# PSUM chunks as one run, a convolution that reads PSUM, and low weight parts kept in DRAM

## The chip, the cores and the metric

One core of one Trainium2 chip. The metric is the device time of one execution in microseconds (us). The engines are named as in the profile: PE (TensorE matmul), PEld (TensorE weight load), DVE (VectorE), ACT (ScalarE), POOL (GpSimd), SP (SyncE, which issues nearly all DMAs here).

## What is computed

One step of a two-layer backbone of width 1024 over 128 context tokens and 1024 latent tokens. Layer 0 mixes tokens by attention and pooling, layer 1 by a Conformer convolution module. Each layer ends with a ConvFFN of inner width 2816: a product with `w_in` (1024 x 5632), a depthwise convolution over three tokens, a gate, a product with `w_out`. All of it is fp32.

```python
def conformer_conv(h, w_pw1, dw_w, dw_b, ln_g, ln_b, w_pw2):
    u = h @ w_pw1
    a, g = jnp.split(u, 2, axis=-1)
    u = a * jax.nn.sigmoid(g)
    u = dwconv(u, dw_w, dw_b)                       # 31 taps
    u = jax.nn.silu(layernorm(u, ln_g, ln_b))
    return u @ w_pw2

def conv_ffn(h, w_in, conv_w, conv_b, w_out):
    u = dwconv(h @ w_in, conv_w, conv_b)            # 3 taps
    a, g = jnp.split(u, 2, axis=-1)
    return (jax.nn.silu(a) * g) @ w_out

for i in range(DEPTH):                              # 2; mc/ml: adaLN shift, scale, gate
    ...
    hl = rmsnorm(xl, norm_mix[i]) * (1 + ml[1]) + ml[0]
    yl = ...                                        # attention + pooling, or conformer_conv
    xl = xl + ml[2] * yl
    hl = rmsnorm(xl, norm_ffn[i]) * (1 + ml[4]) + ml[3]
    xl = xl + ml[5] * conv_ffn(hl, ffn_w_in[i], ffn_conv_w[i], ffn_conv_b[i], ffn_w_out[i])
    # the same for the context tokens xc with mc
```

## The kernel before

Activations lie feature-major: eight tiles `x` of 128 features by 1154 token columns (128 context, a gap of 2, 1024 latent). After layer 0's mixer the work goes over two ranges of columns, A (up to 664 columns) and B (some 490 to 512), each an object of class `Part`. A range of more than 512 columns is cut into `n = 2` equal chunks of `cw` columns, since a matmul writes at most 512 columns here; each chunk begins at the start of its own bank of a two-bank PSUM tile `mm`, so its columns have a hole in the middle. A range of one chunk uses a one-bank tile `mn` where such a pool is open.

Products are exact to about fp32 by splitting: a weight *unit* of 128 x 1024 is loaded as `wraw` by SP, ACT copies it to `whi` in the matmul format fp32r, and POOL subtracts to get the low part `wlo = wraw - whi` (`wunit`, L248 and L249). `wraw` has two buffers, `whi` and `wlo` three. `mm3` then issues three products for each slice: hi x hi (L256), hi x lo (L258), lo x hi (L260). `inproj` makes one such product over eight slices into one PSUM tile.

The feed-forward (`ffn`) runs once for each layer and range. `conv(f)` makes one of 44 inner tiles: ACT evacuates the PSUM tile twice, as a copy `fu` (L1066) and as the middle tap `facc` (L1067), and DVE adds the outer taps from `fu` in SBUF (L1068, L1069). `pair` makes the gated tile: SiLU (L1075), product (L1078: DVE in range A, POOL in range B), hi copy `fh` (L1081, ACT) and low part `fl` (L1082, DVE). `out` takes two gated tiles and two units of `w_out` and goes over eight output tiles; `residual` adds each to `x` by DVE reading PSUM (L428), one instruction for each stretch of columns that `pieces` gives: a stretch ends at the border between context and latent tokens and at the border of a chunk. The order is conv, conv, the output phase of the pair before, conv, conv.

Beside these run other chains, interleaved by generators at written rates: in layer 0's range A the modulation of layer 1 (`mod_beside`: loads `mraw` into one buffer and accumulates on DVE, L314 and L316); in layer 0's range B and in the first part of layer 1's range A the Conformer's 31 taps (`dwconv`: a few taps by ACT and POOL, L963 and L964, the others by DVE, L975) and its gated units (`glu`, L931 to L946). PSUM pools change on the way: three two-bank tiles in layer 0's range A and layer 1's range A, one two-bank and five one-bank tiles in most of layer 0's range B, seven one-bank tiles in layer 1's range B.

Nothing orders engines by hand: the framework's scheduler simulates a timeline and fixes each engine's order, SP's DMAs included, and adds the waits; a tile is free for its next writer when its last reader is done.

## Time and profile before

| | |
|---|---|
| median of 3 runs | 2956.2 us (2955.88 to 2958.3) |
| the profiled execution | 2959.12 us, its span 2957.3 us |
| granted TensorE clock, mean | 0.959 |
| busy: PE, DVE, POOL, ACT | 2702.6, 2088.6, 1428.2, 1162.7 us |
| HBM read, written | 257.36 MB, 12.07 MB |
| L249, the low weight parts (POOL) | 346 instructions, 899.7 us |
| L1068 and L1069, the outer taps (DVE) | 352 instructions, 442.3 us |
| L1066, the copy `fu` (ACT) | 176 instructions, 112.2 us |

Busy times are sums over the span, in which the stages differ; the granted clock is the share of full speed that the TensorE's throttle gave. A group's line in the profile gives count, busy time, mean length of one instruction, and after the bar the idle time just before them with what ended it.

### The profile page before, as it was taken

What the parts mean: (1) busy time and instruction counts of PE and PEld (TensorE: products, weight loads), DVE (VectorE), ACT (ScalarE), POOL (GpSimd) and SP (SyncE); (2) the same over time, 40 slices, a digit from 0 to 9 for tenths busy, and PEclk for the clock granted to TensorE, in tenths of its full rate; (3) what the DMA queues carried; (4) which work ended last, traced back from release to release, by engine and by line L of the source; (5) the groups of instructions that cost most, each with busy time, mean ns of one, the idle gap of its engine ahead of it and who ended that gap; (6) DMA issues with size and microseconds to landing.
All of it is one profiled execution on the core that took longest, in us unless ns stands there. A gap on an engine that the chain in (4) does not pass through costs nothing.

```text
span 2957.3 us, 38873 instructions
## 1 busy us (share of the span) xinstructions
PE 2702.6 (91%) x15108; PEld 2419.7 (82%) x15108; DVE 2088.6 (71%) x2850; ACT 1162.7 (39%) x1807; POOL 1428.2 (48%) x752
## 2 busy tenths in 40 slices
PE   8999997989999999997777799986879999999999
PEld 6798885869998998886666688976778999988887
DVE  3146777677768687859998987679997755754444
ACT  3326665324422332544334243534232423433343
POOL 1313334344423323566657675686563634445554
PEclk9999998989999999998988899998889999999999
DMA  6621225432333333221111222221112222233332
GB/s 244 209 58 59 53 75 154 156 127 80 99 108 107 107 108 121 79 86 57 57 55 60 73 85 79 79 79 44 57 44 73 71 79 82 86 112 100 93 97 88
DMA packets 111897, 271.96 MB, mean 92 GB/s; under 512 B 42849, under 2 KB 48097, under 8 KB 111713
## 3 DMA queue, kind: packets, MB, share of 16 engines
q1 hardware_dynamic: 111712, 269.47, 29.5%
q8 instruction: 120, 1.97, 0.3%
q14 instruction: 65, 0.52, 0.1%
HBM read 257.36 MB, written 12.07 MB: 91 GB/s over the span
## 4 chain that ended last, share of the span: by engine, by line
PE 54%; DVE 34%; DMA 5%; ACT 3%; issue 2%; POOL 2%; SPq 0%; POOLq 0%; DVEq 0%; ACTq 0%
DVE acc L975 13%; PE mm L256 8%; PE mm L258 8%; PE mm L260 8%; PE mn L256 5%; PE mn L258 5%; PE mn L260 5%; DVE modacc L316 4%; DMA mraw<-in_wmod_dram 4%; DVE facc L1068 3%; DVE x L428 3%; DVE facc L1069 2%; PE mm L445 2%; PE O L875 1%; DVE fl L1082 1%
## 5 line engine op out<-in xcount | busy, mean ns | idle before, releaser
L249 POOL TENSOR_TENSOR wlo<-wraw,whi 128x1024 fp32r<-128x1024 f32 x346 | 899.7, 2606 | 1007.9 <-ACT whi L248 815.6
L256 PE MATMUL mm<-h,whi 128*128 128x332 f32 (+6 forms) x2208 | 563.6, 326 | 28.7 <-DVE x L428 9.8
L248 ACT ACTIVATE whi<-wraw 128x1024 fp32r<-128x1024 f32 x348 | 363.1, 1053 | 559.2 <-PE mm L258 262.4
L260 PE MATMUL mm<-h,wlo 128*128 128x332 f32 (+6 forms) x2208 | 564.6, 326 | 9.3 <-POOL wlo L249 9.2
L258 PE MATMUL mm<-h,whi 128*128 128x332 f32 (+6 forms) x2208 | 563.4, 326 | 0.0
L1068 DVE SCALAR_TENSOR_TENSOR facc<-fu,params,facc 128x663 f32<-128x663 f32 (+3 forms) x176 | 262.1, 1489 | 337.6 <-ACT facc L1067 337.6
L975 DVE SCALAR_TENSOR_TENSOR acc<-u,params,acc 128x661 f32<-128x661 f32 (+1 forms) x376 | 484.9, 1312 | 19.2 <-POOL acc L964 15.1
L256 PEld LDWEIGHTS mm<-h,whi 128*128 128x128 f32 x2208 | 385.0, 191 | 47.4 <-issue 25.4
L260 PEld LDWEIGHTS mm<-h,wlo 128*128 128x128 f32 x2208 | 384.5, 190 | 22.9 <-POOL wlo L249 11.4
L258 PEld LDWEIGHTS mm<-h,whi 128*128 128x128 f32 x2208 | 383.2, 190 | 12.2 <-issue 1.7
L428 DVE SCALAR_TENSOR_TENSOR x<-mm,mod,x 128x128 f32<-128x128 f32 (+7 forms) x600 | 233.2, 445 | 70.7 <-PE mm L260 70.0
L260 PE MATMUL mn<-h,wlo 128*128 128x494 f32 (+1 forms) x672 | 262.5, 394 | 15.5 <-POOL wlo L249 15.5
L256 PE MATMUL mn<-h,whi 128*128 128x494 f32 (+1 forms) x672 | 264.6, 394 | 4.8 <-ACT whi L248 4.2
L258 PE MATMUL mn<-h,whi 128*128 128x494 f32 (+1 forms) x672 | 263.8, 393 | 0.0
L256 PE MATMUL mm<-fh,whi 128*128 128x332 f32 (+2 forms) x720 | 180.3, 332 | 65.9 <-ACT fh L1081 32.7
L316 DVE SCALAR_TENSOR_TENSOR modacc<-mraw,sc,modacc 128x512 f32<-128x512 f32 x168 | 173.7, 1086 | 68.8 <-DMA mraw<-in_wmod_dram 68.8
L964 POOL TENSOR_TENSOR acc<-acc,tap 128x508 f32<-128x508 f32 (+1 forms) x104 | 186.3, 1795 | 26.9 <-ACT tap L963 23.8
L1081 ACT ACTIVATE fh<-facc 128x664 fp32r<-128x664 f32 (+3 forms) x88 | 60.4, 686 | 335.0 <-DVE facc L1078 215.2
L256 PEld LDWEIGHTS mm<-fh,whi 128*128 128x128 f32 x720 | 127.0, 198 | 77.3 <-ACT fh L1081 33.9
L258 PE MATMUL mm<-fl,whi 128*128 128x332 f32 (+2 forms) x720 | 178.1, 328 | 9.4 <-DVE fl L1082 9.4
L1069 DVE SCALAR_TENSOR_TENSOR facc<-fu,params,facc 128x663 f32<-128x663 f32 (+3 forms) x176 | 180.2, 1024 | 3.3
L256 PE MATMUL mn<-fh,whi 128*128 128x512 f32 (+1 forms) x336 | 135.0, 420 | 50.2 <-ACT whi L248 24.3
(224 smaller groups left out, 4573.4 us busy)
## 6 DMA issues: line engine op xcount, KB each, us to landing
wraw<-in_fi_dram SPq DMA_DIRECT2D x176, 512.0 KB
mraw<-in_wmod_dram SPq DMA_DIRECT2D x96, 512.0 KB
wraw<-in_fo_dram SPq DMA_DIRECT2D x88, 512.0 KB
wraw<-in_pw_dram SPq DMA_DIRECT2D x48, 512.0 KB
x<-in_x_dram SPq DMA_DIRECT2D x16, 577.0 KB
wraw<-in_woab_dram SPq DMA_DIRECT2D x16, 512.0 KB
wraw<-in_wab_dram SPq DMA_DIRECT2D x12, 512.0 KB
wraw<-in_wv_dram SPq DMA_DIRECT2D x8, 512.0 KB
```

The source lines that it names most:

```text
L248: nc.scalar.activation(hi, raw, AF.Copy)
L249: (eng or nc.gpsimd).tensor_tensor(lo, raw, hi.bitcast(F32), op=ALU.subtract)
L256: mm(pv, whi, xhi[:, a:b], start=start, stop=False)
L258: mm(pv, whi, xlo[:, a:b], start=False, stop=False)
L260: mm(pv, wlo, xhi[:, a:b], start=False, stop=stop)
L316: i = nc.vector.scalar_tensor_tensor(acc, rv, c, acc, op0=ALU.mult, op1=ALU.add)
L428: nc.vector.scalar_tensor_tensor(xd[:, a:b], pv, gate[:, d, st:st + 1], xd[:, a:b], op0=ALU.mult, op1=ALU.add)
L964: nc.gpsimd.tensor_tensor(acc[:, :n], acc[:, :n], p[:, :n], op=ALU.add)
L975: nc.vector.scalar_tensor_tensor(acc[:, :n], u[:, t:t + n], wk(i, t), acc[:, :n], op0=ALU.mult, op1=ALU.add)
L1068: nc.vector.scalar_tensor_tensor(acc[:, 1:W], u[:, 0:W - 1], w(0), acc[:, 1:W], op0=ALU.mult, op1=ALU.add)
L1069: nc.vector.scalar_tensor_tensor(acc[:, 0:W - 1], u[:, 1:W], w(2), acc[:, 0:W - 1], op0=ALU.mult, op1=ALU.add)
L1081: nc.scalar.activation(hi[:, :W], a[:, :W], AF.Copy)
```

## The change

Three things are edited.

1. Chunks as one run. `Part.ps` places the first chunk at the end of bank 0 and the second at the start of bank 1, so that a range's columns lie without a hole; `pieces` then yields one stretch for each stream and no longer cuts at the chunk border. Matmuls still write one chunk each.
2. The convolution reads PSUM. `fu` and its ACT copy go; the two outer taps read the PSUM tile. The tile is free after the second of them.
3. Layer 0's low weight parts are kept. In range A each of the 66 `wlo` units of layer 0 (44 of `w_in`, 22 of `w_out`) is also stored to DRAM; in range B it is loaded from there in place of POOL's subtraction. Layer 1 and all other units are as before.

```diff
     def __init__(self, c0, c1):
         ...
-    def ps(self, t):
-        return t[:, 0, :self.cw] if self.n == 1 else t[:, :self.n, :self.cw]
+    def ps(self, t, s=0, e=None):
+        o = 512 - self.cw if self.n > 1 else 0
+        return t.rearrange("p a b -> p (a b)")[:, o + s:o + (self.w if e is None else e)]
...
     def pieces(self, ps, s, e):
         for st, a, b in self.streams(s, e):
-            for c in range(self.n):
-                o = self.c0 + c * self.cw
-                x, y = max(a, o), min(b, o + self.cw)
-                if x < y:
-                    yield st, ps[:, c, x - o:y - o], x, y
+            yield st, self.ps(ps, a - self.c0, b - self.c0), a, b
...
-    def wunit(self, src, raw=None, eng=None):
+    def wunit(self, src, raw=None, eng=None, keep=None, kept=None):
...
+        if kept is not None:
+            nc.sync.dma_start(lo.bitcast(F32), kept)
         nc.scalar.activation(hi, raw, AF.Copy)
-        (eng or nc.gpsimd).tensor_tensor(lo, raw, hi.bitcast(F32), op=ALU.subtract)
+        if kept is None:
+            (eng or nc.gpsimd).tensor_tensor(lo, raw, hi.bitcast(F32), op=ALU.subtract)
+        if keep is not None:
+            nc.sync.dma_start(keep, lo.bitcast(F32))
         return hi, lo
...
+        def weights(src, store, f):
+            if l:
+                return self.wunit(src[f])
+            return self.wunit(src[f], **{"kept" if s else "keep": store[f]})
+
         def conv(f):
-            (ps,) = self.inproj(part, [self.wunit(wi[f])], H)
-            u = sp.tile([P, self.tw], F32, tag="ft", name=self.nm("fu"))
+            (ps,) = self.inproj(part, [weights(wi, self.lowi, f)], H)
             acc = sp.tile([P, self.tw], F32, tag="ft", name=self.nm("facc"))
             w = lambda t: self.par(f"cw{l}", 3 * f + t)
-            nc.scalar.activation(part.sb(u), part.ps(ps), AF.Copy)
-            nc.scalar.activation(part.sb(acc), part.ps(ps), AF.Identity, bias=self.par(f"cb{l}", f), scale=w(1))
-            nc.vector.scalar_tensor_tensor(acc[:, 1:W], u[:, 0:W - 1], w(0), acc[:, 1:W], op0=ALU.mult, op1=ALU.add)
-            nc.vector.scalar_tensor_tensor(acc[:, 0:W - 1], u[:, 1:W], w(2), acc[:, 0:W - 1],
+            nc.scalar.activation(acc[:, :W], part.ps(ps), AF.Identity, bias=self.par(f"cb{l}", f), scale=w(1))
+            nc.vector.scalar_tensor_tensor(acc[:, 1:W], part.ps(ps, 0, W - 1), w(0), acc[:, 1:W],
+                                           op0=ALU.mult, op1=ALU.add)
+            nc.vector.scalar_tensor_tensor(acc[:, 0:W - 1], part.ps(ps, 1, W), w(2), acc[:, 0:W - 1],
                                            op0=ALU.mult, op1=ALU.add)
             return acc
...
-            units = [self.wunit(wo[f0 + j]) for j in range(2)]
+            units = [weights(wo, self.lowo, f0 + j) for j in range(2)]
...
+            self.lowi = [dp.tile([P, D], F32, name=f"lowi{f}") for f in range(2 * NF)]
+            self.lowo = [dp.tile([P, D], F32, name=f"lowo{f}") for f in range(NF)]
```

(`mm3`, `bcast`, `norm` and `glu` take their PSUM views from `part.ps` in the same way. `s`, in `weights`, is the first output column of the range: 0 in range A.)

The order of instructions around the change. DVE in layer 0's range A, at the start of an output phase, before (`facc` is the last convolution before it, `x` the residual stream, `modacc` the modulation):

```order
L314 TENSOR_SCALAR modacc_7807<-mraw_7942,sc 128x512
L428 SCALAR_TENSOR_TENSOR x_5313<-mm_8094,mod_2_75,x_5313 128x128
L428 SCALAR_TENSOR_TENSOR x_5313<-mm_8094,mod_2_75,x_5313 128x202
L428 SCALAR_TENSOR_TENSOR x_5313<-mm_8094,mod_2_75,x_5313 128x330
L1068 SCALAR_TENSOR_TENSOR facc_8066<-fu_8065,params,facc_8066 128x663
L428 SCALAR_TENSOR_TENSOR x_5314<-mm_8110,mod_2_75,x_5314 128x128
L428 SCALAR_TENSOR_TENSOR x_5314<-mm_8110,mod_2_75,x_5314 128x202
L428 SCALAR_TENSOR_TENSOR x_5314<-mm_8110,mod_2_75,x_5314 128x330
L1069 SCALAR_TENSOR_TENSOR facc_8066<-fu_8065,params,facc_8066 128x663
```

And in the changed kernel at the same place:

```order
L317 TENSOR_SCALAR modacc_7833<-mraw_7966,sc 128x512
L1075 SCALAR_TENSOR_TENSOR facc_8089<-mm_8040,params,facc_8089 128x663
L432 SCALAR_TENSOR_TENSOR x_5379<-mm_8118,mod_2_141,x_5379 128x128
L432 SCALAR_TENSOR_TENSOR x_5379<-mm_8118,mod_2_141,x_5379 128x532
L1077 SCALAR_TENSOR_TENSOR facc_8089<-mm_8040,params,facc_8089 128x663
L432 SCALAR_TENSOR_TENSOR x_5380<-mm_8133,mod_2_141,x_5380 128x128
L432 SCALAR_TENSOR_TENSOR x_5380<-mm_8133,mod_2_141,x_5380 128x532
```

The taps now read `mm`, each stands one residual earlier, and a residual is two instructions.

SP in layer 0's range A, before, with the engines whose semaphores a DMA waits for (`in_fi` holds the units of `w_in`, `in_fo` those of `w_out`):

```order
L239 DMA wraw_6466<-in_fi_dram 128x1024 [waits DMAHW1_49,Pool_49]
L239 DMA wraw_6531<-in_fi_dram 128x1024 [waits DMAHW3_49,Pool_49]
L239 DMA wraw_6600<-in_fi_dram 128x1024 [waits DMAHW5_49,Pool_49]
L239 DMA wraw_6665<-in_fi_dram 128x1024 [waits DMAHW6_49,Pool_49]
L239 DMA wraw_6734<-in_fo_dram 128x1024 [waits DMAHW7_49,Pool_49]
```

And now (`lowi` is the kept copy in DRAM):

```order
L251 DMA lowi_73<-wlo_6394 128x1024 [waits Pool_49]
L235 DMA wraw_6522<-in_fi_dram 128x1024 [waits DMAHW1_49,Activation_49]
L251 DMA lowi_95<-wlo_6457 128x1024 [waits Pool_49]
L235 DMA wraw_6586<-in_fi_dram 128x1024 [waits DMAHW3_49,Activation_49]
L251 DMA lowi_74<-wlo_6525 128x1024 [waits Pool_49]
L235 DMA wraw_6654<-in_fi_dram 128x1024 [waits DMAHW6_49,Activation_49]
```

A store stands ahead of each load and has taken over its wait for POOL.

POOL in layer 0's range B, between one gate product and the next, before (`sum` and `acc` belong to the depthwise convolution):

```order
L1078 TENSOR_TENSOR facc_13015<-facc_13015,facc_13060 128x494
L964 TENSOR_TENSOR acc_12979<-acc_12979,tap_13461 128x661
L937 MEMSET u_13182 128x15 x2
L249 TENSOR_TENSOR wlo_13244<-wraw_13241,whi_13243 128x1024
L986 TENSOR_TENSOR sum_12646<-sum_12646,acc_12659 128x661
L249 TENSOR_TENSOR wlo_13293<-wraw_13290,whi_13292 128x1024
L249 TENSOR_TENSOR wlo_13299<-wraw_13296,whi_13298 128x1024
L249 TENSOR_TENSOR wlo_13344<-wraw_13341,whi_13343 128x1024
L1078 TENSOR_TENSOR facc_13228<-facc_13228,facc_13273 128x494
```

And now:

```order
L1086 TENSOR_TENSOR facc_12921<-facc_12921,facc_12964 128x494
L941 MEMSET u_13085 128x15 x2
L990 TENSOR_TENSOR sum_12558<-sum_12558,acc_12571 128x661
L249 TENSOR_TENSOR wlo_13242<-wraw_13239,whi_13241 128x1024
L1086 TENSOR_TENSOR facc_13129<-facc_13129,facc_13172 128x494
```

Only the subtraction of a gated unit is left of the four; those of the feed-forward's units have become loads on SP.

More of the change, by code (lines that the diff above doesn't have):

```diff
@@ L82, in __init__ @@
         self.cw = self.w // self.n
-    def ps(self, t):
-        return t[:, 0, :self.cw] if self.n == 1 else t[:, :self.n, :self.cw]
-    def sb(self, t):
-        return t[:, :self.w] if self.n == 1 else t[:, :self.w].rearrange("p (a b) -> p a b", a=self.n)
+    def ps(self, t, s=0, e=None):
+        o = 512 - self.cw if self.n > 1 else 0
+        return t.rearrange("p a b -> p (a b)")[:, o + s:o + (self.w if e is None else e)]
     def streams(self, s, e):
@@ L253, in mm3 @@
         mm = self.nc.tensor.matmul
-        cs = [(ps[:, c, :part.cw], off + c * part.cw, off + (c + 1) * part.cw) for c in range(part.n)]
+        cs = [(part.ps(ps, c * part.cw, (c + 1) * part.cw), off + c * part.cw, off + (c + 1) * part.cw)
+              for c in range(part.n)]
         for pv, a, b in cs:
@@ L383, in bcast @@
                 if x < y:
-                    mm(ps[:, c, x - a:y - a], lhs, self.cst("id")[:, x - o:y - o], start=True, stop=True)
+                    mm(part.ps(ps, x - part.c0, y - part.c0), lhs, self.cst("id")[:, x - o:y - o],
+                       start=True, stop=True)
     def norm(self, part, xs, g, sh, H, tp, halo=None, gap=1):
@@ L409, in norm @@
             t = tp.tile([P, self.tw], F32, tag="ft", name=self.nm("nt"))
-            nc.vector.tensor_tensor(part.sb(t), part.ps(rb), part.sb(xs[k][:, c0:c1]), op=ALU.mult)
+            nc.vector.tensor_tensor(t[:, :W], part.ps(rb), xs[k][:, c0:c1], op=ALU.mult)
             for s, a, b in part.streams(c0, c1):
@@ L930, in glu @@
         sg = sp.tile([P, UW], F32, tag="s", name=self.nm("sg"))
-        nc.scalar.activation(part.sb(sg), part.ps(pg), AF.Sigmoid)
+        nc.scalar.activation(sg[:, :part.w], part.ps(pg), AF.Sigmoid)
         yield
@@ L945, in glu @@
             nc.vector.tensor_copy(u[:, 0:31], self.halo[:, i, 0:31])
-            nc.vector.tensor_tensor(u[:, 31:31 + part.w], pa[:, 0, :part.w], sg[:, :part.w], op=ALU.mult)
+            nc.vector.tensor_tensor(u[:, 31:31 + part.w], part.ps(pa), sg[:, :part.w], op=ALU.mult)
         self.us.append(u)
```

## Prediction

> **What bounds the kernel now.** I read the page's busy shares and slices first, then cut the span into stages with the view of windows, then asked in the bad stages which line the time goes to.
>
> ```profile
> PE 2702.6 (91%) x15108; PEld 2419.7 (82%) x15108; DVE 2088.6 (71%) x2850; ACT 1162.7 (39%) x1807; POOL 1428.2 (48%) x752
> ...
> PE   8999997989999999997777799986879999999999
> ...
> DVE  3146777677768687859998987679997755754444
> ```
>
> PE is the bound in most slices (74 us each). It isn't in slices 18 to 22 and in some of 26 to 30, where DVE shows its nines. By stage:
>
> ```profile
> core 0: us, PE busy (x) PEld busy (x) DVE busy (x) ACT busy (x) POOL busy (x), PEclk, DMA share, GB/s
> 678.00:1195.00 517.00, 500.05 (x3198) 483.41 (x3197) 391.61 (x559) 176.27 (x221) 178.64 (x78) 0.99 0.33 104
> 1195.00:1340.00 145.00, 139.11 (x712) 121.83 (x710) 103.69 (x116) 73.09 (x100) 91.20 (x48) 0.99 0.26 77
> 1340.00:1740.00 400.00, 312.05 (x1448) 266.37 (x1449) 371.80 (x333) 146.15 (x187) 254.19 (x123) 0.89 0.21 63
> 1740.00:1815.00 75.00, 67.46 (x318) 56.10 (x317) 61.30 (x76) 35.98 (x54) 59.57 (x38) 0.98 0.25 78
> 1815.00:1990.00 175.00, 165.44 (x901) 149.35 (x900) 111.42 (x120) 76.75 (x103) 123.86 (x73) 0.99 0.27 82
> 1990.00:2240.00 250.00, 191.12 (x1138) 185.03 (x1137) 245.95 (x292) 85.65 (x113) 144.58 (x64) 0.86 0.17 49
> 2240.00:2560.00 320.00, 318.77 (x2046) 309.99 (x2045) 201.34 (x300) 117.86 (x150) 143.13 (x69) 1.00 0.25 76
> 2560.00:2957.00 397.00, 388.86 (x1713) 315.93 (x1711) 196.95 (x234) 151.07 (x207) 197.65 (x93) 1.00 0.32 98
> ```
>
> Rows: layer 0's feed-forward over range A; three rows over range B (the Conformer's depthwise convolution beside it in 1340:1740); the pointwise stage; layer 1's feed-forward over A (depthwise convolution beside it until 2240) and over B. DVE is full, 93% and 98%, in 1340:1740 and 1990:2240; there PE sits idle 88 and 59 us and the granted clock falls to 0.89 and 0.86. PE's need comes from the full stages: a 332-column matmul takes 500.05/3198 = 0.156 us, a 512-column one 388.86/1713 = 0.227. In 1340:1740:
>
> ```profile
> L256 PE MATMUL mn<-h,whi 128*128 128x494 f32 x192 | 76.2, 397 | 4.2 <-ACT whi L248 4.2
> ...
> L256 PE MATMUL mm<-h,whi 128*128 128x332 f32 x190 | 46.5, 327 | 8.7 <-ACT sg L931 6.4 <-DVE u L940 2.4
> ...
> L256 PE MATMUL mn<-fh,whi 128*128 128x494 f32 x92 | 42.6, 476 | 40.5 <-ACT whi L248 22.9 <-DVE x L428 13.1 <-ACT facc L1067 4.4
> ```
>
> Three products each: 852 narrow and some 570 wide, 852 x 0.227 + 570 x 0.156 = 282 us against 400. The `whi` named as releaser isn't slow itself; ACT stood before it, waiting for DVE:
>
> ```profile
> ACT L1075 <- DVE facc L1069: 60.6, 6, 13.9
> ```
>
> Why DVE is full, same window, and then the spread (min/median/max) of three lines over the whole run:
>
> ```profile
> L975 DVE SCALAR_TENSOR_TENSOR acc<-u,params,acc 128x661 f32<-128x661 f32 x180 | 266.7, 1495 | 2.6
> ...
> L1068 DVE SCALAR_TENSOR_TENSOR facc<-fu,params,facc 128x493 f32<-128x493 f32 x24 | 30.3, 1263 | 15.6 <-ACT facc L1067 15.6
> L1069 DVE SCALAR_TENSOR_TENSOR facc<-fu,params,facc 128x493 f32<-128x493 f32 x23 | 22.1, 960 | 0.1
> ```
> ```profile
> L249 POOL TENSOR_TENSOR wlo<-wraw,whi 128x1024 fp32r<-128x1024 f32 x48 | 140.1, 2925 | 56.4 <-ACT whi L248 56.2 <-POOL sum L986 0.2
> L964 POOL TENSOR_TENSOR acc<-acc,tap 128x661 f32<-128x661 f32 x41 | 83.6, 2039 | 17.2 <-ACT tap L963 15.8
> ```
> ```profile
> L1068 DVE SCALAR_TENSOR_TENSOR facc<-fu,params,facc x176: 719/1748/3039, 689.0 to 2941.8; 128x663 f32<-128x663 f32 x44, 128x493 f32<-128x493 f32 x44, 128x647 f32<-128x647 f32 x44, 128x511 f32<-128x511 f32 x44
> ```
> ```profile
> L428 DVE SCALAR_TENSOR_TENSOR x<-mn,mod,x x168: 711/732/751, 1231.1 to 2952.5; 128x510 f32<-128x510 f32 x88, 128x492 f32<-128x492 f32 x80
> ```
>
> The same operation on about 500 columns takes 711 to 751 ns when one operand lies in PSUM (L428), never more, and 719 to 3039 when both lie in SBUF (L1068): it is held up by about the length of a POOL instruction. So DVE's time in the full windows is work plus waiting inside the instruction for POOL, and POOL's largest item there is the subtraction L249.
>
> **The change, part by part.** The sum starts from the profiled execution, 2959.1 us (span 2957.3), 2.9 above the median 2956.2.
>
> *Convolution from PSUM, window 1340:1740.* The unhindered length on 493 columns is 719 ns. Saved: 24 x (1263 - 719) = 13 us and 23 x (960 - 719) = 6 us.
>
> Two unhindered groups of the whole run, which the next steps use as lengths:
>
> ```profile
> L428 DVE SCALAR_TENSOR_TENSOR x<-mn,mod,x 128x510 f32<-128x510 f32 x88 | 61.8, 740 | 7.9 <-PE mn L260 7.9
> ...
> L1069 DVE SCALAR_TENSOR_TENSOR facc<-fu,params,facc 128x663 f32<-128x663 f32 x44 | 39.9, 906 | 1.1
> ```
>
> *No subtraction in layer 0's range B.* Of the 48 units in the window 24 are convolutions (L1068 x24) and 92/8 = 11.5 are output units (8 matmuls of L256 each): 35.5 x 2.925 = 104 us of POOL's 254 go, 41%. The depthwise taps L975 are unhindered at about 905 ns: L1069 in layer 0's range A, where POOL seldom meets it, needs 906 for 663 columns. Their hold-up is 180 x (1495 - 905) = 106 us; with 41% less of POOL, 43 us less. Bounds: 0 (the remaining POOL work meets DVE as often) to 106. DVE falls to 371.8 - 62 = 310 us, still above PE's 282; at the same 93% fullness the window lasts 333 us: **-67**. The other rows of range B are nearly full on PE: **-3**.
>
> *Window 1990:2240.* POOL's subtractions stay (layer 1). What goes is the convolutions' hold-up and one of three residual pieces:
>
> ```profile
> L1068 DVE SCALAR_TENSOR_TENSOR facc<-fu,params,facc 128x647 f32<-128x647 f32 x18 | 27.3, 1515 | 0.0
> L1069 DVE SCALAR_TENSOR_TENSOR facc<-fu,params,facc 128x647 f32<-128x647 f32 x18 | 20.1, 1118 | 0.0
> L428 DVE SCALAR_TENSOR_TENSOR x<-mm,mod,x 128x320 f32<-128x320 f32 x29 | 15.6, 537 | 0.0
> ...
> L428 DVE SCALAR_TENSOR_TENSOR x<-mm,mod,x 128x194 f32<-128x194 f32 x29 | 11.7, 405 | 0.0
> ```
>
> At 890 ns for 647 columns (906 less 16 columns of 1 ns): 18 x 625 + 18 x 228 = 15 us; with one piece of 514 columns at 744 ns, 29 x (537 + 405 - 744) = 6 us. Together **-21** (bounds -10, if DVE waits for PE instead, and -45).
>
> [...]
>
> *What the later release of PSUM costs.* Before, ACT's two passes (L1066, L1067) freed a convolution's tile; now DVE's second tap does. In range A tiles have two banks and there are three. An output phase takes one per 12 x 0.156 = 1.9 us, so its third needs the tile of the last convolution:
>
> ```profile
> 855.86 0.71 ACT L1066 ACTIVATE fu<-mm 128x664 f32<-128x664 f32 x1
> ...
> 856.46 0.90 ACT L1067 ACTIVATE facc<-mm,params 128x664 f32<-128x664 f32 x1
> ...
> 856.96 1.16 DVE L428 SCALAR_TENSOR_TENSOR x<-mm,mod,x 128x128 f32<-128x128 f32 x3 [3.38 <-PE mm L260]
> ...
> 858.03 1.12 DVE L1068 SCALAR_TENSOR_TENSOR facc<-fu,params,facc 128x663 f32<-128x663 f32 x1
> ...
> 858.58 0.47 PE L256 MATMUL mm<-fh,whi 128*128 128x332 f32 x2
> ```
>
> The last row is the third output tile, which starts without a wait. By the new order DVE does tap, residual of the first output tile, tap. ACT's single pass ends at 856.8, the first tap (0.9) at 857.7, the residual (two pieces, 1.05) at 858.7, the second tap at 859.6: 1.1 us later than now. Where ACT comes later or DVE waits for `mraw` it is 3 us or more. I take 1.5 us for the 11 output phases of 678:1195 and 1.2 us for the 4 in 2240:2560 that directly follow a convolution: **+21** (bounds 0 and 22 x 5). In the full window 1990:2240 DVE has depthwise taps to do meanwhile, so nothing is added; range B has five narrow tiles and one phase needs the last convolution's only for its fifth output tile, 4 x 6 x 0.227 = 5.4 us on.
>
> *66 stores in 678:1195.* On SP a store waits for POOL's subtraction, which the load behind it waited for before, so no new wait; it adds 512 KB each, 67 GB/s to the 104 there, and can delay the landing of `mraw`:
>
> ```profile
> DVE modacc L316 <- DMA mraw<-in_wmod_dram: 50.5, 22, 4.9
> ```
>
> Half the longest wait more on each would be 54 us of DVE's 125 idle us, nothing is the other bound; I take **+5** for PE.
>
> The 66 kept loads in range B wait for PE to leave the slot (there are three), as the subtraction did. A load of that size lands within
>
> ```profile
> 868.41 3.58 DMA mraw<-in_wmod_dram
> ...
> 1020.16 5.48 DMA wraw<-in_fi_dram
> ```
>
> in the chain of waits, and at least one unit of 24 x 0.227 = 5.4 us runs between the slot's release and its next use: I cost them at nothing, covered by that unit. If the cover is a few us short, PE waits at its third matmul, the first that reads `wlo` (a rival below).
>
> *The end.* The chain of waits closes with one `fu` pass of the last convolution, which goes: **-1**.
>
> ```profile
> 2940.53 0.60 ACT fu L1066
> ```
>
> Sum -67 - 3 - 21 + 21 + 5 - 1 = -66: 2893 on the profiled execution, **2890** against the median.
>
> **Rivals.**
> - *PE sets the pace everywhere.* If POOL's removal frees most of the 106 us, 1340:1740 falls to PE's 282 plus little (-110) and 1990:2240 loses 35; with +15 and -5 that is 2821. For it: PE's clock in these windows would rise too. Against: POOL keeps 150 us of other work there. [...]
> - *The kept loads become the wait.* They queue on SP behind raw loads that wait for POOL's gated-unit subtractions; 3 us late at each of 11 output phases of range B is +33: 2923.
> - *Slower: the wide ring.* If each of the 22 wide output phases loses more than 4.2 us (DVE caught behind an `mraw` wait, then two taps), 93 us eat the gain; at 5 us the time is 2979. Against: DVE is 24% idle in range A.
> - *DVE's relief doesn't reach PE:* another link of POOL, ACT and DVE sets the window, 2955.
>
> **How the numbers follow.** Forecast 0.52 (its own range 2865 to 2915), PE's pace 0.15, kept loads 0.17, wide ring 0.10, no relief 0.06. Faster by over 0.2% (what a measurement can tell): the first three, 0.84; within, 0.06; slower, 0.10. The range 2815 to 2945 leaves out the last two and the low tail of the second.
>
> **What would show it.** Convolution taps flat at 720 to 910 ns; POOL's subtractions 66 fewer; 1340:1740's work in about 333 us with DVE near 310 and PE's clock above 0.89; 678:1195 longer by 10 to 30 us with PE waiting for `facc` at the third output tile. Wrong would be a range B that keeps its length with PE waiting for a DMA of `wlo`, or a range A longer by 60.

## The result, and the profile after

The changed kernel takes 2855.97 us (median of four runs, 2854.53 to 2859.94) against 2956.04 us: a ratio of 0.9666, 95% interval 0.9649 to 0.9683. Run again later it gave 0.9658 (0.9645 to 0.9672). The forecast was 2890, so the gain is 100 us where 66 were expected. 2856 lies within the range stated as a whole (2815 to 2945), 9 us below the forecast's own (2865 to 2915), about as far from 2890 as from the 2821 of the rival with PE's pace. The profiled execution has a span of 2858.2 us at a mean granted clock of 0.965.

The page after, busy shares and slices:

```profile
PE 2675.8 (94%) x15108; PEld 2410.5 (84%) x15108; DVE 1875.1 (66%) x2634; ACT 1072.4 (38%) x1631; POOL 1225.7 (43%) x686
...
PE   8999998889999999999798999987789999999999
...
DVE  3146777577667767658989856499994644644444
```

The run of sevens and eights on PE in the middle is nearly gone; the one in slices 27 to 30 (layer 1's range A, where DVE shows nines) is not. By stage, cut as near to the rows of before as the changed order allows:

```profile
core 0: us, PE busy (x) PEld busy (x) DVE busy (x) ACT busy (x) POOL busy (x), PEclk, DMA share, GB/s
669.60:1186.90 517.30, 502.31 (x3195) 486.81 (x3194) 358.42 (x478) 149.56 (x175) 172.65 (x75) 0.98 0.52 172
1186.90:1331.00 144.10, 140.69 (x738) 125.44 (x737) 88.64 (x120) 70.28 (x90) 53.52 (x35) 1.00 0.43 145
1331.00:1640.00 309.00, 272.87 (x1348) 240.88 (x1347) 285.04 (x303) 126.62 (x150) 141.61 (x82) 0.93 0.40 131
1640.00:1721.50 81.50, 81.50 (x395) 70.11 (x394) 45.18 (x70) 39.52 (x56) 32.22 (x29) 1.00 0.53 175
1721.50:1896.50 175.00, 165.47 (x901) 149.35 (x900) 111.29 (x113) 76.03 (x102) 124.91 (x74) 0.99 0.27 82
1896.50:2143.00 246.50, 193.84 (x1151) 187.16 (x1149) 243.94 (x272) 76.70 (x99) 133.07 (x65) 0.86 0.17 50
2143.00:2461.00 318.00, 317.83 (x2035) 308.44 (x2035) 164.28 (x239) 103.81 (x126) 140.47 (x68) 1.00 0.26 77
2461.00:2858.00 397.00, 388.94 (x1712) 315.78 (x1710) 175.92 (x226) 129.03 (x161) 192.13 (x93) 1.00 0.32 98
```

The three rows of layer 0's range B hold the same work together (2478 matmuls before, 2481 now) and went from 620 us to 534.6. Most of that is in the one that DVE filled, 400 to 309, with PE's granted clock up from 0.89 to 0.93. Not all of the 91 us is a gain: the row holds 1348 matmuls where 1448 stood, and the others went to the rows beside it. At the fourth row's 81.5/395 = 0.206 us each they are an estimated 21 us, which leaves about 70 for this row and 15 for the two beside it. The row of layer 1's range A hardly moved (250 to 246.5) and DVE is as full as before. In the third row, DVE's depthwise taps and convolution taps, and POOL's subtractions:

```profile
L979 DVE SCALAR_TENSOR_TENSOR acc<-u,params,acc 128x661 f32<-128x661 f32 x172 | 211.3, 1239 | 2.8
L1075 DVE SCALAR_TENSOR_TENSOR facc<-mn,params,facc 128x493 f32<-128x493 f32 x20 | 14.5, 725 | 7.3 <-ACT facc L1074 7.3
L1077 DVE SCALAR_TENSOR_TENSOR facc<-mn,params,facc 128x493 f32<-128x493 f32 x20 | 14.5, 723 | 0.0
```
```profile
L249 POOL TENSOR_TENSOR wlo<-wraw,whi 128x1024 fp32r<-128x1024 f32 x11 | 29.4, 2673 | 38.3 <-ACT whi L247 38.3
```

The taps, which read PSUM now, are flat at 725 ns (1263 and 960 before), a depthwise tap fell from 1495 to 1239 ns, and 11 subtractions stand where 48 did.

### The profile page after: what moved, and what is told of

Same layout as the page of the kernel before. It is cut to its first block, busy times and chain, and to the rows that moved or that the text cites. A ratio compares the mean times of both kernels' runs of the same rounds, so it can differ in the third digit from the quotient of the medians.

```text
span 2858.2 us, 38636 instructions
## 1 busy us (share of the span) xinstructions
PE 2675.8 (94%) x15108; PEld 2410.5 (84%) x15108; DVE 1875.1 (66%) x2634; ACT 1072.4 (38%) x1631; POOL 1225.7 (43%) x686
## 4 chain that ended last, share of the span: by engine, by line
PE 67%; DVE 24%; DMA 5%; ACT 2%; issue 1%; POOL 1%; SPq 0%; POOLq 0%; DVEq 0%; ACTq 0%
DVE acc L979 11%; PE mm L259 11%; PE mm L263 10%; PE mm L261 10%; PE mn L259 7%; PE mn L261 7%; PE mn L263 7%; DVE modacc L319 3%; DMA mraw<-in_wmod_dram 3%; PE mm L449 2%; DVE x L432 2%; PE O L879 1%; DVE facc L1075 1%; PE ms L479 1%; DVE facc L1077 1%
## 5 line engine op out<-in xcount | busy, mean ns | idle before, releaser
L249 POOL TENSOR_TENSOR wlo<-wraw,whi 128x1024 fp32r<-128x1024 f32 x280 | 701.0, 2509 | 1033.0 <-ACT whi L247 777.1
L979 DVE SCALAR_TENSOR_TENSOR acc<-u,params,acc 128x661 f32<-128x661 f32 (+1 forms) x376 | 451.4, 1222 | 13.4 <-POOL acc L968 8.7
L432 DVE SCALAR_TENSOR_TENSOR x<-mm,mod,x 128x128 f32<-128x128 f32 (+7 forms) x408 | 210.1, 559 | 86.1 <-PE mm L263 73.6
L1075 DVE SCALAR_TENSOR_TENSOR facc<-mm,params,facc 128x663 f32<-128x663 f32 (+3 forms) x92 | 81.8, 889 | 190.5 <-ACT facc L1074 190.5
L319 DVE SCALAR_TENSOR_TENSOR modacc<-mraw,sc,modacc 128x512 f32<-128x512 f32 x168 | 165.7, 1041 | 61.7 <-DMA mraw<-in_wmod_dram 61.4
L1075 DVE SCALAR_TENSOR_TENSOR facc<-mn,params,facc 128x493 f32<-128x493 f32 (+1 forms) x84 | 61.9, 737 | 200.6 <-ACT facc L1074 200.3
L263 PE MATMUL mm<-fh,wlo 128*128 128x332 f32 (+2 forms) x720 | 177.2, 327 | 2.5 <-POOL wlo L249 2.5
L259 PEld LDWEIGHTS mm<-fh,whi 128*128 128x128 f32 x720 | 127.9, 199 | 60.8 <-issue 40.4
```

Source lines behind the costliest of these rows:

```text
L249: (eng or nc.gpsimd).tensor_tensor(lo, raw, hi.bitcast(F32), op=ALU.subtract)
L259: mm(pv, whi, xhi[:, a:b], start=start, stop=False)
L263: mm(pv, wlo, xhi[:, a:b], start=False, stop=stop)
L319: i = nc.vector.scalar_tensor_tensor(acc, rv, c, acc, op0=ALU.mult, op1=ALU.add)
L432: nc.vector.scalar_tensor_tensor(xd[:, a:b], pv, gate[:, d, st:st + 1], xd[:, a:b], op0=ALU.mult, op1=ALU.add)
L979: nc.vector.scalar_tensor_tensor(acc[:, :n], u[:, t:t + n], wk(i, t), acc[:, :n], op0=ALU.mult, op1=ALU.add)
```

## The experiments

Both kernels and the twelve runs, with the span of each profiled execution cut at the same four PE events: the end of layer 0's mixer output projection (its 490-column matmuls), the end of the last modulation group ("A" is layer 0's range A up to there), the first 492-column matmul of layer 1's second gated-unit part ("B" is layer 0's range B and the pointwise stage up to there), and the last variance group of layer 1's convolution norm ("1A", which holds layer 1's range A). Times in us; the ratio is to the kernel before.

| kernel | median | ratio (95%) | start | A | B | 1A | rest |
|---|---|---|---|---|---|---|---|
| before | 2956.0 | 1 | 673.9 | 518.7 | 706.5 | 419.4 | 638.8 |
| changed | 2856.0 | 0.9666 (0.9649 to 0.9683) | 665.4 | 519.0 | 621.2 | 414.5 | 638.1 |
| e9_again (changed) | 2855.4 | 0.9658 (0.9645 to 0.9672) | 667.6 | 511.4 | 621.4 | 414.5 | 637.7 |
| e3_run | 2951.3 | 0.9991 (0.9982 to 1.0001) | 668.0 | 522.2 | 705.3 | 420.2 | 638.3 |
| e1_psum | 2907.6 | 0.9842 (0.9824 to 0.9860) | 659.8 | 504.8 | 684.9 | 414.6 | 637.9 |
| e2_keep | 2873.7 | 0.9721 (0.9704 to 0.9737) | 673.7 | 522.8 | 623.2 | 419.3 | 638.3 |
| e4_l1load | 2810.8 | 0.9513 (0.9492 to 0.9534) | 667.4 | 511.8 | 621.4 | 366.4 | 635.5 |
| e5_fuA0 | 2870.2 | 0.9719 (0.9706 to 0.9733) | 661.6 | 529.5 | 618.2 | 416.1 | 637.8 |
| e6_nostore | 2844.9 | 0.9637 (0.9624 to 0.9650) | 663.2 | 505.7 | 621.0 | 414.2 | 638.0 |
| e7_noload | 2848.9 | 0.9650 (0.9636 to 0.9665) | 665.2 | 522.1 | 609.8 | 415.0 | 637.8 |
| e8_tb | 2879.1 | 0.9755 (0.9741 to 0.9770) | 667.6 | 525.2 | 621.5 | 470.9 | 605.0 |
| e10_defer | 2858.2 | 0.9664 (0.9651 to 0.9678) | 664.7 | 520.1 | 620.2 | 413.9 | 637.9 |
| e11_prep | 2852.9 | 0.9646 (0.9633 to 0.9660) | 671.2 | 550.1 | 620.6 | 376.0 | 636.5 |
| e12_prep11 | 2849.9 | 0.9648 (0.9633 to 0.9662) | 670.6 | 535.8 | 621.3 | 390.1 | 636.7 |

B and 1A repeat within about 3 us wherever their code is the same; A and the start don't, and the first experiment says how far.

### The yardstick: the changed kernel again

No edit.

> The changed kernel itself once more, unchanged: the yardstick for differences of 5 to 15 us between its variants, since layer 0's range A took 519.0 us in its profiled execution and 511.8 us in that of the variant with loads for layer 1, which is the same kernel up to there. Theory A (an execution's range A differs by up to some 8 us by itself): total 2850 to 2862, range A anywhere between 510 and 521. Rival B (519 was usual and 511.8 was the exception): range A 517 to 521.

It took 2855.4 us with an A of 511.4. Over the executions whose code is that of the changed kernel in range A, A is 511.4, 511.8, 519.0, 522.1 and 525.2 (e9_again, e4_l1load, changed, e7_noload, e8_tb), and 520.1 in e10_defer, where SP's order comes out the same: theory A, and the spread is wider than it said. A difference of less than 14 us in a single A means nothing by itself, one of 5 us in B or 1A does.

### The parts alone: layout, convolution, kept parts

The run layout alone (e3_run): the changed kernel with ACT's copy and the taps on it back, and without keeping.

```diff
+            u = sp.tile([P, self.tw], F32, tag="ft", name=self.nm("fu"))
...
+            nc.scalar.activation(u[:, :W], part.ps(ps), AF.Copy)
...
-            nc.vector.scalar_tensor_tensor(acc[:, 1:W], part.ps(ps, 0, W - 1), w(0), acc[:, 1:W], ...)
+            nc.vector.scalar_tensor_tensor(acc[:, 1:W], u[:, 0:W - 1], w(0), acc[:, 1:W], ...)
```

> Part 1 alone: the chunks of a part as one run in PSUM, one instruction where there were two or three; the convolution still copies PSUM to SBUF and its taps read the copy. Theory A: nothing that bounds a stage changes: within 8 us of before, 2948 to 2964. Rival: joining the instructions alone saves DVE's fixed time per instruction in the stages that DVE bounds: 2920 to 2945.

Ratio 0.9991: theory A. Fewer, longer DVE instructions alone are worth at most some 5 us (0.9982, the low end of the interval).

Layout and convolution from PSUM, no keeping (e1_psum):

```diff
-            return self.wunit(src[f], **{"kept" if s else "keep": store[f]})
+            return self.wunit(src[f])
```

> Parts 1 and 2 alone: the chunks lie as one run and the feed-forward convolution reads PSUM; all low weight parts are still subtracted on POOL. Theory A (the gain is DVE's relief from POOL, and hold-up that the taps shed is taken up by the depthwise convolution beside them as long as POOL has as much to do): layer 0's range B gives 10 to 30 us, layer 1's range A 0 to 5, total 2925 to 2950. In the stretch that answers to 1340:1740 of before the taps run flat (710 to 770 ns for the narrow forms) and the depthwise multiply-add's mean rises above the 1312 ns of before. Rival B (the convolution's operands alone made the gain, the kept parts nothing): 2855 to 2875. Rival C (hold-ups simply add: the taps' excess of 52 us in range B and 15 in layer 1's range A both go): about 2890.

2907.6 us lies in none of the three ranges, 17 us under theory A's: against e3_run B fell by 20 (705.3 to 684.9) and 1A by 6, about as theory A said, but A fell by 17 as well and the start by 8, which none had.

The keeping alone, put into the kernel before (e2_keep):

```diff
+        if kept is not None:
+            nc.sync.dma_start(lo.bitcast(F32), kept)
...
+        if keep is not None:
+            nc.sync.dma_start(keep, lo.bitcast(F32))
```

> Part 3 alone, on the kernel before: layer 0's low weight parts are stored by the first range and loaded by the second; the layout of PSUM and the convolution from its copy in SBUF stay. Theory A: POOL loses 66 subtractions in layer 0's range B, about 41% of its work there, and both the depthwise convolution (106 us of hold-up) and the taps (52 us) shed that share: 43 + 21 = 64 us, less 0 to 5 for stores, total 2885 to 2905, the larger part of the whole change's 100 us. Rival B (only the convolution's operands count): 2945 to 2960. Rival C (with the taps still reading SBUF, the loads and the remaining subtractions hold DVE up as before): 2930 to 2960.

2873.7 us, 11 under theory A's range: B fell by 82 or 83 where 64 were priced. Where the parts overlap is read in DVE's lines of B up to the convolution norm's first sums. Before:

```profile
L975 DVE SCALAR_TENSOR_TENSOR acc<-u,params,acc 128x661 f32<-128x661 f32 x192 | 281.0, 1476 | 5.8 <-POOL acc L964 3.0
L1068 DVE SCALAR_TENSOR_TENSOR facc<-fu,params,facc 128x493 f32<-128x493 f32 x32 | 42.0, 1312 | 30.2 <-ACT facc L1067 30.2
L1069 DVE SCALAR_TENSOR_TENSOR facc<-fu,params,facc 128x493 f32<-128x493 f32 x32 | 37.3, 1167 | 0.4
```

Taps from PSUM, all subtractions there (e1_psum):

```profile
L979 DVE SCALAR_TENSOR_TENSOR acc<-u,params,acc 128x661 f32<-128x661 f32 x192 | 290.1, 1523 | 7.7 <-POOL acc L968 4.7
L1075 DVE SCALAR_TENSOR_TENSOR facc<-mn,params,facc 128x493 f32<-128x493 f32 x30 | 21.7, 724 | 0.2
L1073 DVE SCALAR_TENSOR_TENSOR facc<-mn,params,facc 128x493 f32<-128x493 f32 x30 | 21.7, 723 | 26.1 <-ACT facc L1072 26.0
```

Kept parts, taps from SBUF (e2_keep):

```profile
L981 DVE SCALAR_TENSOR_TENSOR acc<-u,params,acc 128x661 f32<-128x661 f32 x192 | 229.1, 1205 | 6.9 <-POOL acc L970 3.9
L1079 DVE SCALAR_TENSOR_TENSOR facc<-fu,params,facc 128x493 f32<-128x493 f32 x30 | 32.9, 1096 | 19.5 <-ACT facc L1078 19.4
L1080 DVE SCALAR_TENSOR_TENSOR facc<-fu,params,facc 128x493 f32<-128x493 f32 x30 | 28.5, 949 | 0.2
```

Both (e9_again), and the whole stretch of these four kernels, in this order:

```profile
L979 DVE SCALAR_TENSOR_TENSOR acc<-u,params,acc 128x661 f32<-128x661 f32 x192 | 234.8, 1232 | 3.3
```
```profile
1222.90:1725.00 502.10, 408.26 (x1926) 349.82 (x1925) 442.75 (x385) 196.46 (x252) 323.83 (x159) 0.91 0.23 66
```
```profile
1196.80:1673.10 476.30, 398.71 (x1888) 346.93 (x1887) 414.51 (x373) 180.42 (x219) 307.50 (x156) 0.90 0.22 68
```
```profile
1226.80:1639.70 412.90, 376.27 (x1857) 330.09 (x1857) 354.01 (x375) 191.89 (x246) 193.93 (x112) 0.95 0.40 133
```
```profile
1211.30:1620.30 409.00, 372.99 (x1851) 330.68 (x1850) 344.96 (x367) 177.63 (x215) 188.66 (x111) 0.94 0.40 134
```

Taps from PSUM shed their whole hold-up (1312 and 1167 ns to 724), but with POOL as busy as before (308 us of 476, 324 of 502 before) the depthwise taps took 9 us of it back (281.0 to 290.1). Less POOL work (324 us to 194) lifts both, and once that is done the convolution from PSUM adds only 4 us to this stretch: 412.9 to 409.0. The gain of range B is POOL's, as the forecast had it; the two parts don't add (20 + 82 against 84 together).

Not all of it goes through DVE. PE's waits for the low part itself in this stretch, two lines before and one in e9_again:

```profile
PE mn L260 <- POOL wlo L249: 21.0, 7, 5.4
PE mm L260 <- POOL wlo L249: 8.8, 4, 2.6
```
```profile
PE mm L263 <- POOL wlo L249: 8.0, 2, 4.4
```

So some 22 us less of PE's waiting is a shorter way from POOL to PE, which the prediction didn't price. It was 25 us in e1_psum and 8 in e2_keep, so it went with the kept parts.

### What holds layer 1's range A up

The low parts of that range too are loaded (e4_l1load):

```diff
             if l:
-                return self.wunit(src[f])
+                return self.wunit(src[f], kept=None if s else store[f])
```

> The changed kernel, and layer 1's range A also loads its low parts (it reads those that layer 0 stored, so the numbers of layer 1 differ) in place of subtracting them on POOL. It tells whether POOL's work is what holds layer 1's range A up, where the change gave 3.5 us of the 21 forecast. Theory A (the taps' hold-up moved to the depthwise convolution because POOL's work there stayed): the window that answers to 1896.5:2143 of the changed kernel falls from 246.5 to 200 to 220 us, depthwise hold-up from 64 to under 40 us; total 2820 to 2840. Rival B (DVE is bound there by its own work, or the pace rule sets the length): the window falls by under 8 us, total 2848 to 2858. Rival C (the loads come late, each as a wait of PE's weight load): total over 2858.

1A fell by 48 us and the whole to 2810.8, more than theory A's 2820 to 2840. Together with the two later runs that load 11 and 22 of the 66 units there, the stretch from the last 492-column matmul to the variance group shows a series. First the changed kernel (e9_again), then 11 (e12_prep11), 22 (e11_prep) and all units (e4_l1load) loaded; for each the row of the stretch and of DVE's depthwise taps in it:

```profile
1865.90:2214.90 349.00, 287.17 (x1770) 279.78 (x1770) 302.43 (x343) 110.56 (x141) 189.66 (x94) 0.89 0.19 56
```
```profile
L979 DVE SCALAR_TENSOR_TENSOR acc<-u,params,acc 128x508 f32<-128x508 f32 x173 | 196.2, 1169 | 1.1
```
```profile
1893.20:2217.80 324.60, 284.20 (x1768) 278.21 (x1769) 278.40 (x342) 110.74 (x139) 157.23 (x83) 0.92 0.24 75
```
```profile
L997 DVE SCALAR_TENSOR_TENSOR acc<-u,params,acc 128x508 f32<-128x508 f32 x172 | 172.0, 1041 | 0.6
```
```profile
1907.40:2217.90 310.50, 279.77 (x1770) 274.78 (x1770) 260.20 (x342) 110.84 (x139) 132.88 (x72) 0.93 0.30 97
```
```profile
L997 DVE SCALAR_TENSOR_TENSOR acc<-u,params,acc 128x508 f32<-128x508 f32 x172 | 155.8, 950 | 0.4
```
```profile
1866.20:2167.00 300.80, 276.11 (x1770) 271.54 (x1770) 251.37 (x342) 111.07 (x139) 89.64 (x55) 0.95 0.38 130
```
```profile
L979 DVE SCALAR_TENSOR_TENSOR acc<-u,params,acc 128x508 f32<-128x508 f32 x172 | 147.0, 899 | 1.6 <-POOL acc L968 1.2
```

As POOL's busy time goes 190, 157, 133, 90 us, one and the same DVE instruction goes 1169, 1041, 950, 899 ns, DVE's time 302, 278, 260, 251, PE's clock 0.89, 0.92, 0.93, 0.95, and the stretch 349.0, 324.6, 310.5, 300.8. DVE's own work is unchanged over the row (342 or 343 instructions). PE hardly waits for POOL's low part directly here; in the changed kernel's stretch it is this line alone:

```profile
PE mm L263 <- POOL wlo L249: 2.3, 1, 2.3
```

That POOL's work sets this stretch through DVE is shown; rivals B and C are out.

### The wide ring and the convolution in layer 0's range A

ACT's copy and the taps from SBUF come back in that range alone (e5_fuA0):

```diff
+            if l == 0 and s == 0:
+                u = sp.tile([P, self.tw], F32, tag="ft", name=self.nm("fu"))
+                ...
+                nc.scalar.activation(u[:, :W], part.ps(ps), AF.Copy)
+                ...
```

> The changed kernel with the convolution from a copy in SBUF, as before, in layer 0's range A alone; everything else as changed. Theory A (the later release in the wide ring of three costs the 16 us forecast there, and something else made it good): layer 0's range A gets shorter by 10 to 20 us, total 2836 to 2848. Theory B (reading PSUM shortens that range by what the copies and held-up taps cost, more than the ring takes, as parts 1 and 2 alone had 504.8 us from the end of its first norm to the last modulation group where the run layout alone had 522.2): the range gets longer by 5 to 17 us, total 2860 to 2874. Rival C: neither counts there, within 4 us: 2852 to 2860.

Theory B: the whole takes 15 us more by the medians, 16 to 18 by the ratios, and A is 529.5 us against 511 to 525 with the convolution from PSUM. In A, PE's wait for the last reader of a convolution's tile, in the kernel before, in e5_fuA0 and in the changed kernel (e9_again):

```profile
PE mm L256 <- ACT facc L1067: 5.1, 3, 3.1
```
```profile
PE mm L259 <- ACT facc L1077: 10.1, 4, 3.1
```
```profile
PE mm L259 <- DVE facc L1077: 1.1, 1, 1.1
```

The release by ACT's second pass, with another pass ahead of it, made PE wait for 5.1 and 10.1 us; the release by DVE's second tap for 1.1. The later release, which the forecast priced at 16 us here, isn't there. Of the 18 us between the two profiles' A, 529.5 and 511.4, PE's waits make up 12 (23.1 against 10.7 in all); the rest is PE's own busy time, 506.4 against 500.7 us, and where that comes from wasn't traced.

### Stores and kept loads

Two stores in place of 66 (e6_nostore):

```diff
-            return self.wunit(src[f], **{"kept" if s else "keep": store[f]})
+            if s:
+                return self.wunit(src[f], kept=store[0])
+            return self.wunit(src[f], keep=store[0] if f == 0 else None)
```

> The changed kernel with 2 stores of low parts in place of 66; layer 0's range B loads these two everywhere, so its numbers differ, while loads, POOL's work and DVE's stay the same. Theory A (the stores of range A cost more than the 5 us forecast, since that range takes 519.0 us with them and 504.8 without them in the run of parts 1 and 2): layer 0's range A falls by 8 to 15 us, total 2840 to 2848. Theory B (5 us as forecast): 2849 to 2853. Rival C (the two spans differ by chance from run to run, stores are free): within 3 us of the changed kernel, 2853 to 2860.

2844.9 us, theory A: the stores cost 11 us by the medians, 6 to 9 by the ratios, and A is 505.7 us against 511 to 525. In range A, DVE's wait for the modulation's loads, without the stores and then with them (the changed kernel's first execution), and PE's wait for DVE's residual likewise:

```profile
DVE modacc L319 <- DMA mraw<-in_wmod_dram: 35.5, 21, 3.6
DVE modacc L319 <- DMA mraw<-in_wmod_dram: 44.2, 22, 4.6
```
```profile
PE mm L259 <- DVE x L432: 4.3, 4, 2.3
PE mm L259 <- DVE x L432: 12.0, 5, 4.1
```

One pair of executions proves little in A, but the others agree. With the convolution from PSUM, the two kernels without stores (e1_psum, e6_nostore) have 33.7 and 35.5 us for the first wait, 4.8 and 4.3 for the second and an A of 504.8 and 505.7; the six executions with them have 40.1 to 46.8, 7.9 to 14.5 and 511.4 to 525.2. That fits the way that the forecast named, a later landing of `mraw`. It isn't shown to be the only one: with the copy in SBUF the first wait is 50.5 and 42.7 us without stores (before, e3_run) and 36.5 and 56.2 with them (e2_keep, e5_fuA0). SP waits for POOL about as long with the stores as without, 258.7 us at the loads in e6_nostore and 245.3 at the stores in e9_again, 51 times each.

An attempt to issue each store behind the next unit's load:

```diff
         if keep is not None:
-            nc.sync.dma_start(keep, lo.bitcast(F32))
+            self.held.append((keep, lo))
```

> The changed kernel with each store of a low part issued one unit later: behind the load of the next raw weights in SP's queue in place of ahead of it, where it waits for POOL's subtraction. All 66 stores and all loads remain. Theory A (the stores cost 11 to 13 us because the next loads, of weights and of the modulation matrix, stand behind a store that waits): layer 0's range A falls to 505 to 510 us, total 2843 to 2850. Rival B (what costs is the writes themselves: traffic and DVE's slower operations, 361 us busy in range A with stores and 354 without): within 4 us of the changed kernel, total 2852 to 2860.

2858.2 us, but this says nothing for rival B: the scheduler put the held stores back ahead of the loads, so SP's order in this kernel is that of the changed one:

```order
L246 DMA lowi_73<-wlo_6394 128x1024 [waits Pool_49]
L236 DMA wraw_6521<-in_fi_dram 128x1024 [waits DMAHW1_49,Activation_49]
L246 DMA lowi_95<-wlo_6457 128x1024 [waits Pool_49]
L236 DMA wraw_6585<-in_fi_dram 128x1024 [waits DMAHW3_49,Activation_49]
```

The run counts as one more repetition. Whether another place for the stores would be cheaper stays open.

Without the loads of the kept copies (e7_noload):

```diff
+            if s:
+                raw = self.wload(src[f])
+                ...
+                nc.scalar.activation(hi, raw, AF.Copy)
+                return hi, hi
```

> The changed kernel without the 66 loads of the kept copies: layer 0's range B multiplies the high part in their place, so its numbers differ; the stores stay. Theory A (the loads land before PE needs them and cost nothing, as forecast): from layer 0's range B to the first glu of layer 1's second part within 5 us of the 588.9 us of the changed kernel, total 2850 to 2860. Rival B (the loads hold the raw weights up in their queue, or come late now and then): that stretch falls by 8 to 25 us, total 2832 to 2848.

The median, 2848.9, is just under theory A's range and just over rival B's low one; B fell by 11.6 us (621.4 to 609.8), which is rival B. The ratio (0.9650 against 0.9658 and 0.9666) puts the loads at 2 to 5 us, with intervals that overlap, the medians at 7, B at 12: small, and by B alone not nothing. No wait of PE for these loads shows in the changed kernel's range B. The trace points at rival B's queue: ACT waits 30.6 us for raw units of `w_in` there with the loads and 12.3 without, and PE 16.0 us for ACT's high parts against 6.2. But without the loads the buffers of `wlo` stand free as well, so how they cost it isn't settled.

### Attempts at a faster version

A lower pace of the depthwise convolution beside layer 1's range A (e8_tb):

```diff
-TB = 3.5
+TB = 2.75
```

> The changed kernel with the pace of the depthwise convolution beside layer 1's range A lowered from 3.5 to 2.75 steps a turn (one number). Theory A (DVE bounds that stretch with 243.9 of 246.5 us busy while the stretch behind it has DVE busy for about half): PE keeps going and the work moves to where DVE has room, total 2830 to 2848. Rival B (the output projection and the norm behind the depthwise convolution come late and their rest runs alone at the end of range A): 2856 to 2885. Rival C (nothing: the order only shifts who waits): 2850 to 2860.

2879.1 us: in rival B's range. The changed kernel's stretch up to the last depthwise tap, and that of e8_tb:

```profile
1865.90:2134.20 268.30, 206.50 (x1226) 199.34 (x1226) 266.37 (x288) 82.06 (x106) 149.25 (x74) 0.85 0.17 52
```
```profile
1879.80:2148.10 268.30, 206.47 (x1226) 199.34 (x1226) 266.41 (x288) 82.22 (x106) 149.20 (x74) 0.86 0.17 52
```

The same length, matmuls and instructions: the scheduler packed the taps at the lower pace as at the higher one, so DVE got no relief. The number moves only what comes behind, the pointwise output and the last norm, to a later place, and 24 us are lost there (1A and the rest together 1075.9 against 1052.2). Which waits make them up wasn't traced.

Then two versions that compute low parts of layer 1's range A ahead of time, beside layer 0's range A, where PE is full and POOL a third busy (502 and 173 us of 517 in the changed kernel; e11_prep with 22 units, e12_prep11 with 11):

```diff
+    def prep(self):
+        ...
+            raw = self.wload(src)
+            lo = self.wp.tile([P, 1024], F32R, tag="wlo", name=self.nm("wlo"), bufs=self.wbufs)
+            self.nc.scalar.activation(lo, raw, AF.Copy)
+            self.nc.gpsimd.tensor_tensor(lo, raw, lo.bitcast(F32), op=ALU.subtract)
...
+            if l == s == 0 and f % 2 == 0:
+                self.prep()
             g = conv(NF + f)
+            if l == s == 0 and f % 2:
+                self.prep()
```

> A version meant to beat both: the stores deferred as in e10_defer, and beside layer 0's range A, where PE is busy for 97% and POOL for a third, the low parts of the first 22 weight units of layer 1's range A are subtracted on POOL (two more for each group of the feed-forward) and stored; layer 1's range A loads them. All numbers are those of the reference. Theory A (with all 66 units loaded layer 1's range A fell by 48 us, nearly all of it in the stretch of its first 35 units: 22 of 35 give 25 to 30; 22 loads, subtractions and stores beside layer 0's range A cost 0 to 10): total 2822 to 2840. Rival B (the extra units take buffers and places in SP's queue ahead of the units that PE waits for; layer 0's range A grows by 20 us and more): 2850 to 2880. Rival C (the gain needs all units, since DVE stays the bound with those left): 2840 to 2858.

> As e11_prep, with 11 units in place of 22, one for each group of layer 0's range A, behind the second gate convolution alone. All numbers are those of the reference. In e11_prep layer 1's range A fell from 349.0 to 310.5 us (1.75 us a unit) and layer 0's range A grew from 511.4 or 519.0 to 550.1. Theory A (both scale with the units, the cost faster than that since each extra unit stood ahead of one that PE waited for): layer 1's range A falls by 17 to 22 us, layer 0's range A grows by 6 to 14, total 2840 to 2850. Rival B (the cost is one of traffic and POOL's time and scales as the gain does): total 2850 to 2860, no difference from the changed kernel.

1A gained more than expected, 38.5 and 24.4 us, and range A gave it back: 550.1 and 535.8 us against 511 to 525. In e11_prep's range A PE waits for the low parts of its own units:

```profile
PE mm L281 <- POOL wlo L252: 14.7, 13, 1.7
```

This wait is 5.9 us in e12_prep11 and under 1 us in the changed kernel, so it comes with the extra units on POOL. It is a part of the 25 to 39 us that range A lost; the rest wasn't taken apart.

With 0.9646 (0.9633 to 0.9660) and 0.9648 (0.9633 to 0.9662) neither can be told from the changed kernel. For e11_prep that is rival B, for e12_prep11 the border of both theories: gain and cost shrank alike. What e4_l1load shows is on offer, some 45 us, needs a place for this work that PE doesn't wait on; none was found here.

## Why the prediction was right, and where its terms were off

*The bound.* DVE, held up by POOL, sets the two full windows: shown by the two rows of four kernels, one for each window; in layer 0's some 22 us went from POOL to PE directly. One and the same depthwise tap took 1169 ns beside 190 us of POOL work and 899 ns beside 90 (e9_again, e4_l1load), while taps with one operand in PSUM stayed at 723 to 726 ns with POOL busy for 308 us of 476 (e1_psum) and for 189 of 409 (e9_again). By what path POOL lengthens a DVE instruction was not shown.

*Layer 0's range B, -70.* It gave 85 (rows of windows) or 84 (e3_run to e9_again in B). The depthwise term was right: 41% less hold-up of 1495 - 905 ns makes 1253, and 1239 came out; and the window's -67 is close to the estimate of 70 for the same matmuls. Too small were the rows beside it, -3: in the stretch from range B's start to the norm's sums DVE fell by 98 us (442.75 to 344.96), 46 of them depthwise taps and 36 convolution taps (some 5 of these are four taps that now fall outside the stretch), where the forecast had priced only the convolution taps inside its window, at 19. PE's direct waits for the low part, 22 us less, had no term. And PE's clock was higher where its idle time was shorter, 0.91 with 93.8 us idle and 0.94 with 36.0: 408.26/1926 = 212 ns a matmul to 372.99/1851 = 202.

*Layer 1's range A, -21: gave 3.5 to 5.* The step that failed is that DVE's saved time was put down as time of the stage. The stretch to the last depthwise tap, before:

```profile
1964.60:2251.00 286.40, 217.97 (x1311) 211.68 (x1312) 281.96 (x327) 98.12 (x129) 168.28 (x76) 0.87 0.18 52
2251.00:2318.50 67.50, 67.50 (x459) 67.50 (x458) 42.16 (x58) 28.31 (x39) 36.44 (x18) 1.00 0.23 71
```

It was 286.4 and is 268.3 us, so 18 us did go. But in it PE did 1226 matmuls where it had done 1311: the new order sets about the same taps (174 and 173) beside fewer matmuls, PE's idle time fell by only 6 us (68.4 to 61.8), and the 85 matmuls follow in the part where PE is full. A depthwise tap got slower meanwhile (1098 ns to 1169), as in e1_psum's range B. Two of PE's waits over both parts, before and then in the changed kernel (e9_again):

```profile
PE mm L256 <- ACT fh L1081: 28.8, 3, 13.5
PE mm L256 <- ACT facc L1067: 8.7, 2, 4.4
```
```profile
PE mm L259 <- DVE facc L1077: 16.8, 7, 4.3
PE mm L259 <- ACT fh L1089: 3.4, 1, 3.4
```

DVE's relief let the gated tiles come sooner, but PE now waits 16.8 us for the second tap to free a convolution's tile. This is the wide ring's later release, in the very window for which the forecast added nothing because DVE has other work there. That work stands in the way: in the six waits of over 1 us one or two depthwise taps run on DVE between the first tap and the second. The wait shrinks as POOL's work goes (13.9, 6.1 and 5.4 us with 11, 22 and all units loaded). No run separates it from the rest.

*The wide ring, +21: in layer 0's range A a gain.* In e5_fuA0 and in e3_run against e1_psum the convolution from PSUM shortens range A, by 15 to 18 us in the runs' times and in the pair of profiles. The third output tile does start later, 4.46 us after the last convolution before and 5.1 to 5.5 now (mean of ten phases), but the eighth at 15.1 before and 15.1 to 15.8 now; and the third is at 4.6 in e1_psum and e6_nostore, so most of its lateness goes with the stores. The forecast had counted the tap that comes later and not the ACT pass that goes: PE's 5 to 10 us of waiting for `facc` of ACT.

*Stores, +5: 6 to 11. Kept loads, 0: 2 to 12.* Near in size; the stores' mechanism fits the traces, that of the loads is open.

*Not in the sum:* the first 674 us, in which only part 1 of the change acts, came out 6 to 9 us shorter. The two executions with the old layout have 673.9 and 673.7, the twelve with the new one 659.8 to 671.2. That speaks for a small gain, but no experiment was made on it.

By stages, the forecast's -66 was -70 in range B, -16 in layer 1's range A with its share of the ring, +21 in range A with the stores, -1 at the end. The two profiled executions gave -85, -5, between 0 and -7, and -1, with -6 to -9 at the start: 99 and 105 in all. So the bound and the largest term were right, while two terms of equal size, -21 and +21, were both wrong, with errors that ran against each other; that 2890 came within 34 us is in part luck. The rival with PE's pace (2821) had its direction right; it failed where it needed layer 1's window to fall by 35 and range B by over 110. The kept loads as a wait of 33 us, the ring as a loss of the whole gain and no relief at all are out.

## What to carry to other kernels

Where an engine is full, compare the same instruction's duration in quiet and busy stretches (899 and 1169 ns here): what it loses to another engine is a term of its own. When some of the held-up instructions were relieved here, the rest were held up more (1476 to 1523 ns, e1_psum); with the other engine's work taken away they were held up less (1205 ns, e2_keep), which is the surer way. Count the next engine's instructions in the stretch before and after: in layer 1's range A the stretch that DVE fills got 18 us shorter and the stage only 3.5 to 5, since 1226 matmuls stood in it where 1311 had. Under a scheduler, look at the order before believing that a pace or a moved line did anything.

## What was not expected

PE's granted clock went with its gaps: over the four kernels of the series PE was idle for 61.8, 40.4, 30.7 and 24.7 us of the stretch, the clock was 0.89, 0.92, 0.93 and 0.95, and PE's time for the same 1770 or so matmuls went from 287.2 to 276.1 us, 11 of the 48 us gained. And layer 0's range A, in an unchanged kernel, varied from 511 to 525 us while the stages behind it repeated within 2 us; a difference of that size in that stage needs the medians, not one profile.
